# Paired weight chunks ordered by raw tile, and one reciprocal for two query blocks, in a hybrid convolution and attention layer

## The chip, the cores and the metric

The kernel runs on one core of a Trainium2 chip. A core has a matrix engine (TensorE, PE in the profile; its weight loads are shown apart as PEld), a vector engine (VectorE, DVE), a scalar engine (ScalarE, ACT), GpSimd (POOL), and SyncE (SP), which here only issues transfers (DMA). The metric is the time of one execution on the device in microseconds (us); lower is better.

## The reference

One layer over 512 latent tokens and 256 context tokens of width 1024, in float32. The input is normalised and modulated (h for the latent tokens, hc for the context), and one projection makes ten parts of width 1024:

```
parts = split(h @ w_in)            # b, c, x, z_a | q, k, v, z_b | g_a, g_b
y_a = (silu(z_a) * b * conv3(c * x)) @ w_out_conv
p   = softmax(concat([q.k_window * scale + bias, q.k_ctx * scale]))
y_b = (silu(z_b) * (p @ [v_window, v_ctx])) @ w_out_attn
y   = (sigmoid(g_a) * y_a + sigmoid(g_b) * y_b) @ w_o
out = x + gt * rmsnorm(y)
```

There are 16 heads of 64 channels. Each query sees a window of 8 x 16 grid positions and all context keys in one softmax.

## The kernel before

**Precision by splitting.** TensorE works on a rounded float type. Each operand is therefore split (`split`, line 64) into a high half, a cast on ScalarE (line 67), and the remainder, a subtraction on VectorE (line 68). A product is three matmuls: high by high, high by low, low by high.

**Weights.** A chunk of the input projection is 1024 x 256. It is loaded as two raw tiles of 512 KB (`Chunk`, line 84), the first with the rows 0 to 511, the second with the rows 512 to 1023. SP issues the two loads in this order (line 87). There are three buffers for raw tiles (`bufs=3`), so while one chunk has two of them, the next one can have only one of its tiles loaded; its other load waits until a buffer is free. The split halves go into tiles `w` (four buffers).

**Paired chunks.** Sixteen of the chunks are multiplied by a scheme with seven half-size products in place of eight. With b11 and b12 the left and right columns of the first raw tile, and b21 and b22 those of the second, it needs the splits of B11 = b11, B21 = b21, B22 = b22 and of four sums: T1 = b11 + b12, T2 = T1 + b22, T3 = b12 + b22, T4 = b21 + T2. The sums are made in place in the raw tiles: T1 and then T2 over b11, T4 over b21, T3 over b12. `first()` (line 96) does the four sums and splits B11, B21, T1 and T2. `second()` (line 110) splits T4, T3 and B22. T3 is the last that lies in the first raw tile; T4 and B22 lie in the second. `pair` (line 267) multiplies in the order B11, B21, T1, T2 (with A11, A12, X1, S2), then `chunk.more()` starts `first()` of the next paired chunk, and then T4, T3, B22 (with A22, S3, S4). Line 262 is every matmul of these products. Paired are the gate chunks zb 0 to 2, the convolution chunks cx and bz from 5 on, and all merge gates g but g2.

**Attention.** For each of 8 head pairs p, two heads h and four blocks b of 128 queries, `scores` (line 653) multiplies queries and keys (lines 664, 673), adds the bias and takes the extreme of the row (line 680, VectorE), then ScalarE takes the exponential with the sum of the row in z (line 686), VectorE the reciprocal of z (line 687), and ScalarE scales the block with it (line 688). Two blocks at a time, `turn2` (line 691) transposes them on TensorE (line 695) and splits them into TH and TL. `gather` (line 699) multiplies the four blocks of a head with the values (line 714).

**Order.** The loop at line 789 goes over the 64 blocks. In each step it takes some parts of the projections and gates of the plan (line 192) as filling for TensorE, then the scores two blocks ahead, and in every odd block the transposes of two. So the scores of a block stand in the program two steps ahead of its place, and the transposes of a pair stand behind its odd block. Outside the first stage (lines 405 to 514) the order on each engine is not written out by hand: it is planned when the program is built, from the order of the program and assumed durations of the instructions and transfers, and an engine then takes its queue in the planned order.

Of the kernel before, what the change touches and what calls it, by code (L numbers as in the profile page):

```python
# [9 lines left out]
F32 = mybir.dt.float32  # L10
F32R = mybir.dt.float32r
AF = mybir.ActivationFunctionType
# [3 lines left out]
P = 128  # L16
# [11 lines left out]
def layer(ctx: ExitStack, tc, xp, ctxt, ctxT, cc, wmod, small, wfirst, win, wout, wo, rel, tab, out):  # L28
    nc = tc.nc
# [34 lines left out]
    def split(H, L, src, scale=None):  # L64

        if scale is None:
            nc.scalar.copy(H, src)  # L67
            nc.vector.tensor_sub(L, src, H.bitcast(F32))  # L68
        else:
            nc.scalar.mul(H, src, scale)  # L70
            nc.vector.scalar_tensor_tensor(
                out=L, in0=src, scalar=scale, in1=H.bitcast(F32), op0=ALU.mult, op1=ALU.subtract
            )
# [4 lines left out]
    def wtile(shape):  # L78
        return wp.tile(shape, F32R, name="w", bufs=4)

    class Chunk:
# [14 lines left out]
        def first(self):  # L96
            (b11, b12), (b21, b22) = self.b = [(r[:, :, :P], r[:, :, P:]) for r in self.raws]
            t, sums = (wtile([P, 2, 2, 4, P]) for _ in range(2))
            for x, b in ((t[:, 0], b11), (t[:, 1], b21)):
                split(x[:, 0], x[:, 1], b)  # L100
            nc.vector.tensor_add(b11, b11, b12)
            split(sums[:, 0, 0], sums[:, 0, 1], b11)
            nc.vector.tensor_add(b11, b11, b22)
            split(sums[:, 1, 0], sums[:, 1, 1], b11)
            nc.vector.tensor_add(b21, b21, b11)
            nc.vector.tensor_add(b12, b12, b22)
            self.B = {"B11": t[:, 0], "B21": t[:, 1], "T1": sums[:, 0], "T2": sums[:, 1]}
            return self

        def second(self):  # L110
            t, last = (wtile([P, 2, 2, 4, P]) for _ in range(2))
            for n, x, b in (("T4", t[:, 0], self.b[1][0]), ("T3", t[:, 1], self.b[0][1]), ("B22", last[:, 0], self.b[1][1])):
                split(x[:, 0], x[:, 1], b)
                self.B[n] = x

# [151 lines left out]
    def pair(c1, c2):  # L267

        w = chunk().B
        a, b, e = (pj()[:, :256] for _ in range(3))  # L270
        first, second = slice(0, 256), slice(256, S)
        product(a, A11, w["B11"], True)
        nc.scalar.copy(c1[:, first], a)
        product(b, A12, w["B21"], True)
        product(e, blocks_h["X1"], w["T1"], True)
        nc.scalar.copy(c2[:, second], e)
        product(a, blocks_h["S2"], w["T2"], False)
        nc.scalar.copy(c2[:, first], a)
        nc.vector.tensor_add(c1[:, first], c1[:, first], b)  # L279
        chunk.more()  # L280
        yield
        product(b, A22, w["T4"], True)
        product(a, blocks_h["S3"], w["T3"], False)
        nc.scalar.copy(c1[:, second], a)
        product(e, blocks_h["S4"], w["B22"], False)
        for cols, x in ((second, c1[:, second]), (first, e)):
            nc.vector.scalar_tensor_tensor(
                out=c2[:, cols], in0=c2[:, cols], scalar=-1.0, in1=x, op0=ALU.mult, op1=ALU.subtract
            )
        nc.vector.tensor_add(c1[:, second], c1[:, second], b)  # L290
# [35 lines left out]
    with ExitStack() as p0:  # L326
# [44 lines left out]
        raws, first = {}, {}  # L371
# [33 lines left out]
        with tc.manual_schedule(engines={E.PE, E.DVE, E.Activation, E.SP}):  # L405
# [74 lines left out]
            for k in range(KT):  # L480
# [9 lines left out]
                m = st.tile([P, S], F32, name="m", bufs=2)  # L490
# [95 lines left out]
    aw = pa.enter_context(tc.tile_pool(name="aw", bufs=2, reuse_waits="tile"))  # L586
# [63 lines left out]

    def scores(p, h, b):
        qd, qe, ks = KQ[p]
        if b == 0:
            nc.sync.dma_start(bt[:, 2 * h:2 * h + 2], rel[p, h])
        s = psS()
        qs = slice(b * P, (b + 1) * P)
        if b < 3:

            t = ks[h][:, b * P:(b + 2) * P]
            kt = bass.AP(t.tensor, t.offset, [t.ap[0], [(4 - b) * P, 2], [1, 2 * P]])
            for n, lhs in enumerate((qd[h], qe[h])):
                nc.tensor.matmul(  # L664
                    s.rearrange("p (a c) -> p a c", a=2), lhsT=lhs[:, qs], rhs=kt, start=n == 0, stop=n == 1
                )
        else:
            kt = ks[h].rearrange("p (t c) -> p t c", c=P)
            s4 = s.rearrange("p (t c) -> p t c", c=P)
            n = 0  # L670
            for lhs in (qd[h], qe[h]):
                for o, i in ((slice(0, 2), slice(0, 4, 3)), (slice(2, 4), slice(4, 6))):
                    nc.tensor.matmul(
                        s4[:, o], lhsT=lhs[:, qs], rhs=kt[:, i], start=n == 0, stop=n == 3, skip_group_check=True
                    )
                    n += 1
        e = 2 * h + (b == 3)
        m = aw.tile([P, 1], F32, name="m", bufs=4)
        s3 = s.rearrange("p (a c) -> p a c", a=2)
        nc.vector.tensor_tensor_reduce(  # L680
            out=s3, in0=s3, in1=bt[:, e::4 - e][:, 0:2], scale=-1.0, scalar=3.0e38,
            op0=ALU.add, op1=ALU.min, accum_out=m,
        )
        pt = aw.tile([P, S], F32, name="pt", bufs=3)
        z = aw.tile([P, 1], F32, name="z", bufs=4)
        nc.scalar.activation(pt, s, AF.Exp, bias=m, scale=-1.0, accum_out=z)  # L686
        nc.vector.reciprocal(z, z)  # L687
        nc.scalar.mul(pt, pt, z)  # L688
        return pt

    def turn2(pts, b, TH, TL):
# [91 lines left out]
    pj.tags = (0, 1, 2)  # L783
    blocks = [(p, h, b) for p in range(NPAIR) for h in range(2) for b in range(4)]
    pts = {n: scores(*blocks[n]) for n in range(2)}
    T = None
    sums = block_sums()
    done = 0
    for i, (p, h, b) in enumerate(blocks):
        slot = i % 8  # L790
        if slot == 0:
            items = chain(*(g for g, _ in fill[p]))
            total, done = sum(n for _, n in fill[p]), 0
        if i in (4, 5, 6, 8, 9, 10, 12, 13):
            next(sums)
        upto = -(-total * (slot + 1) // 8)
        while done < upto:
            next(items)
            done += 1
        if T is not None and b == 0:  # L800
            gather(*T)
        if i + 2 < len(blocks):
            pts[i + 2] = scores(*blocks[i + 2])
        if b == 0:
            TH = aw.tile([P, 4, 4, P], F32R, name="TH", bufs=1)
            TL = aw.tile([P, 4, 4, P], F32R, name="TL", bufs=1)
            T = p, h, TH, TL

        if b % 2:
            turn2([pts.pop(i - 1), pts.pop(i)], b - 1, TH, TL)  # L810
# [41 lines left out]
    def quarter(name, pool, tags):  # L852
        return [pool.tile([P, 2, S], F32, name=f"{name}{q}", tag=t) for q, t in enumerate(tags)]
# [28 lines left out]
    for j in range(KT):  # L882
# [17 lines left out]
        if j == 4:  # L900
# [4 lines left out]
            for i in range(2):  # L905
                gb = cv.tile([P, S], F32, name="ta")
                ps = pj()
                for k in range(4):
                    n = 4 * i + k
# [3 lines left out]
        if j == 4:  # L913
            A11, S3 = operand("A11", hp, ("u2", "u3")), operand("S3", hp, ("a2", "a3"))
            for q in range(2):
                split(A11[q][:, 0], A11[q][:, 1], raws[q][:, :, h0])
                x = cv.tile([P, S], F32, name="tb").rearrange("p (k c) -> p k c", k=2)
# [3 lines left out]
            B22, B21, T2, T3 = (quarter(n, hp, (f"h{2 * i}", f"h{2 * i + 1}")) for i, n in enumerate(("B22", "B21", "T2", "T3")))  # L921
# [4 lines left out]
        if j == 6:  # L926
# [6 lines left out]
            T4 = B12  # L933
# [36 lines left out]
    def partial(t, n, first):  # L970
        d = sums[:, t, 3:4]
        if first:
            nc.vector.tensor_scalar(out=d, in0=sums[:, t, n:n + 1], scalar1=0.25 / D, scalar2=EPS, op0=ALU.mult, op1=ALU.add)
        else:
            nc.vector.scalar_tensor_tensor(out=d, in0=sums[:, t, n:n + 1], scalar=0.25 / D, in1=d, op0=ALU.mult, op1=ALU.add)
# [38 lines left out]
    t = [hp.tile([P, 2, S], F32R, name=f"wB22{i}", tag=f"h{2 + i}") for i in range(4)]  # L1014
# [119 lines left out]
```

## Time and profile before

| | us |
|---|---|
| median of 3 runs | 715.55 (715.27 to 716.63) |
| the profiled execution's own time | 715.21 |
| its span in the trace | 713.4 |
| TensorE busy in it | 699.3 |
| VectorE busy | 585.3 |
| ScalarE busy | 425.2 |
| GpSimd busy | 37.6 |

The span runs from the first instruction of the program to the end of the last; 1.8 us of the execution lie outside it. The granted clock of TensorE is 0.998 of the full one. The attention loop runs from about 137 to 512 us of the span, the merge gates from there to about 640 us, and the output product after that. An engine's idle time matters only where TensorE or the end waits for it. In the rows of the profile a line such as L106 is a line of the kernel before; where a helper makes all splits, its line (67 and 68) is told apart by the tiles, as `w<-raw` or `TL<-ps`.

### The profile page before, as it was taken

How to read it: one execution, taken by the hardware profiler on the slowest of the kernel's cores; microseconds unless marked ns; L12 is line 12 of the kernel's file. 1: busy time of each engine (PE TensorE's matmuls, PEld its weight loads, DVE VectorE, ACT ScalarE, POOL GpSimd, SP SyncE). 2: the span in 40 equal slices, each digit the busy share in tenths (PEclk: the TensorE clock that was granted, in tenths of full speed). 3: DMA queues.
4: the chain of work that ended last, by engine and by line, in shares of the span. 5: the costliest groups of instructions: out<-in, count | busy, mean ns of one | idle time of the engine just before them, and what ended most of it. 6: DMA issues, size and time to landing. Idle time of an engine off the chain costs nothing.

```text
span 713.4 us, 11043 instructions
## 1 busy us (share of the span) xinstructions
PE 699.3 (98%) x4052; PEld 614.0 (86%) x4052; DVE 585.3 (82%) x1139; ACT 425.2 (60%) x822; POOL 37.6 (5%) x78
## 2 busy tenths in 40 slices
PE   7999999999999999999999999999999999999996
PEld 4888888888888998898998999998888999988885
DVE  6999999985677897879888698999696675665996
ACT  6575643555476675675866657787673444342563
POOL 0000001120020200201102002000000000000000
PEclk9999999999999999999999999999999999999999
DMA  8996995454260452441563145212832333470013
GB/s 348 406 348 219 288 342 173 97 147 120 74 152 16 111 167 98 92 129 38 134 219 85 27 133 134 92 61 85 283 119 74 105 119 119 161 281 30 30 59 119
DMA packets 34905, 104.06 MB, mean 146 GB/s; under 512 B 4513, under 2 KB 4769, under 8 KB 34850
## 3 DMA queue, kind: packets, MB, share of 16 engines
q1 hardware_dynamic: 28946, 92.20, 37.9%
q0 software_dynamic: 5760, 11.01, 7.3%
q8 instruction: 32, 0.52, 0.3%
q14 instruction: 23, 0.19, 0.1%
q10 hardware_dynamic: 144, 0.13, 0.1%
HBM read 87.07 MB, written 5.24 MB: 129 GB/s over the span
## 4 chain that ended last, share of the span: by engine, by line
PE 89%; DVE 6%; DMA 3%; ACT 1%; issue 1%; DVEq 0%; SPq 0%; ACTq 0%
PE ps L262 17%; PE ps L143 13%; PE ps L144 13%; PE ps L145 13%; PE ps L156 6%; PE ps L941 5%; PE ps L714 4%; PE ps L695 3%; PE ps L161 3%; PE ps L664 2%; DMA raw<-in_win 2%; PE ps L169 2%; DVE w L68 2%; PE ps L397 2%; PE ps L401 2%; PE ps L398 2%
## 5 line engine op out<-in xcount | busy, mean ns | idle before, releaser
L67 ACT CAST w<-raw 128x512 fp32r<-128x512 f32 (+1 forms) x170 | 128.2, 767 | 89.7 <-PE ps L145 45.6
L68 DVE TENSOR_TENSOR w<-raw,w 128x512 fp32r<-128x512 f32 (+1 forms) x170 | 145.6, 866 | 39.5 <-ACT w L67 39.1
L143 PE MATMUL ps<-h,w 128*128 128x512 f32 x272 | 106.8, 392 | 0.0
L145 PE MATMUL ps<-h,w 128*128 128x512 f32 x272 | 106.2, 390 | 0.0
L144 PE MATMUL ps<-h,w 128*128 128x512 f32 x272 | 105.9, 390 | 0.0
L262 PE MATMUL ps<-S,w 128*128 128x256 f32 x768 | 97.4, 283 | 0.0
L262 PEld LDWEIGHTS ps<-S,w 128*128 128x128 f32 x768 | 94.5, 192 | 0.0
L262 PE MATMUL ps<-h,w 128*128 128x256 f32 x576 | 75.2, 284 | 0.2 <-DVE g L279 0.2
L262 PEld LDWEIGHTS ps<-h,w 128*128 128x128 f32 x576 | 71.9, 191 | 1.5 <-DVE g L279 0.5
L145 PEld LDWEIGHTS ps<-h,w 128*128 128x128 f32 x272 | 51.1, 188 | 10.8
L144 PEld LDWEIGHTS ps<-h,w 128*128 128x128 f32 x272 | 51.1, 188 | 10.4
L143 PEld LDWEIGHTS ps<-h,w 128*128 128x128 f32 x272 | 51.1, 188 | 10.3
L686 ACT ACTIVATE pt<-ps,m 128x512 f32<-128x512 f32 x64 | 44.1, 689 | 15.2 <-DVE m L680 14.1
L688 ACT ACTIVATE pt<-pt,z 128x512 f32<-128x512 f32 x64 | 45.8, 725 | 5.2 <-DVE z L687 5.0
L67 ACT CAST TH<-ps 128x512 fp32r<-128x512 f32 x64 | 35.5, 585 | 20.2 <-PE ps L695 20.0
L68 DVE TENSOR_TENSOR TL<-ps,TH 128x512 fp32r<-128x512 f32 x64 | 42.9, 679 | 3.1 <-ACT TH L67 2.9
L680 DVE CUSTOM_DVE_ANT_1 ps<-ps,bt 128x512 f32<-128x512 f32 x56 | 38.7, 694 | 4.1 <-PE ps L664 4.1
L695 PE MATMUL ps<-ident,pt 128*128 128x128 f32 x256 | 33.5, 273 | 0.8 <-DVE TL L68 0.8
L156 PE MATMUL ps<-w,h 128*128 128x512 f32 x128 | 32.5, 395 | 0.0
L695 PEld LDWEIGHTS ps<-ident,pt 128*128 128x128 f32 x256 | 29.2, 140 | 3.3 <-ACT pt L688 1.3
L714 PE MATMUL ps<-TL,V 128*128 128x256 f32 (+1 forms) x96 | 28.2, 323 | 2.4 <-DVE TL L68 2.4
L714 PE MATMUL ps<-TH,V 128*128 128x256 f32 (+1 forms) x96 | 28.5, 319 | 0.0
(247 smaller groups left out, 1337.6 us busy)
## 6 DMA issues: line engine op xcount, KB each, us to landing
raw<-in_win SPq DMA_DIRECT2D x74, 512.0 KB, 4.5
wm<-in_wmod SPq DMA_DIRECT2D x34, 512.0 KB, 6.4
raw<-in_wout SPq DMA_DIRECT2D x16, 512.0 KB, 3.6
bt<-in_rel SPq DMA_DIRECT2D x16, 256.0 KB, 3.4
B<-in_wo SPq DMA_DIRECT2D x8, 512.0 KB, 6.6
fraw<-in_wfirst SPq DMA_DIRECT2D x8, 384.0 KB, 7.9
qd<-qd POOLq DMA_DIRECT2D x24, 128.0 KB, 2.3
qe<-qe POOLq DMA_DIRECT2D x24, 128.0 KB, 3.4
```

Of the source, the lines that this page charges most:

```text
L67: nc.scalar.copy(H, src)
L68: nc.vector.tensor_sub(L, src, H.bitcast(F32))
L143: nc.tensor.matmul(ps, lhsT=H[k][:, cs], rhs=mH[k], start=k == 0, stop=False)
L144: nc.tensor.matmul(ps, lhsT=H[k][:, cs], rhs=mL[k], start=False, stop=False)
L145: nc.tensor.matmul(ps, lhsT=L[k][:, cs], rhs=mH[k], start=False, stop=k == KT - 1)
L156: nc.tensor.matmul(ps, lhsT=mH[k][:, ts], rhs=both[k].rearrange("p a c -> p (a c)"), start=k == 0, stop=False, skip_group_check=True,)
L262: nc.tensor.matmul(ps, lhsT=w[:, x, k], rhs=act[y][k], start=start and k + o == 0, stop=k == 3 and o == 2, skip_group_check=True,)
L680: nc.vector.tensor_tensor_reduce(out=s3, in0=s3, in1=bt[:, e::4 - e][:, 0:2], scale=-1.0, scalar=3.0e38, op0=ALU.add, op1=ALU.min, accum_o ...
L686: nc.scalar.activation(pt, s, AF.Exp, bias=m, scale=-1.0, accum_out=z)
L688: nc.scalar.mul(pt, pt, z)
L695: nc.tensor.transpose(tp[:, c], pt[:, c * P:(c + 1) * P], ident)
L714: nc.tensor.matmul(o3[:, dst], lhsT=V[p][:, kt, h], rhs=src(t), start=n == 0 and t is TH, stop=n == len(work) - 1 and t is TL,)
```

## The change

Three edits. In `first()` the work is ordered by raw tile: B11, the sum T1 and its split come first, then B21, the sum T2 and its split, and the sum for T3 comes ahead of that for T4. In `second()` T3 is split ahead of T4; the products that use them keep their order, T4 first. In `scores` the row sums of an even and the following odd block go into two columns of one tile z. One reciprocal after the odd block's exponential serves both, and then both blocks are scaled one after the other; the even block, which was scaled right after its own exponential, is now scaled there.

```diff
         def first(self):
             (b11, b12), (b21, b22) = self.b = [(r[:, :, :P], r[:, :, P:]) for r in self.raws]
             t, sums = (wtile([P, 2, 2, 4, P]) for _ in range(2))
-            for x, b in ((t[:, 0], b11), (t[:, 1], b21)):
-                split(x[:, 0], x[:, 1], b)
+            split(t[:, 0, 0], t[:, 0, 1], b11)
             nc.vector.tensor_add(b11, b11, b12)
             split(sums[:, 0, 0], sums[:, 0, 1], b11)
+            split(t[:, 1, 0], t[:, 1, 1], b21)
             nc.vector.tensor_add(b11, b11, b22)
             split(sums[:, 1, 0], sums[:, 1, 1], b11)
+            nc.vector.tensor_add(b12, b12, b22)
             nc.vector.tensor_add(b21, b21, b11)
-            nc.vector.tensor_add(b12, b12, b22)
...
         def second(self):
             t, last = (wtile([P, 2, 2, 4, P]) for _ in range(2))
-            for n, x, b in (("T4", t[:, 0], self.b[1][0]), ("T3", t[:, 1], self.b[0][1]), ("B22", last[:, 0], self.b[1][1])):
+            for n, x, b in (("T3", t[:, 0], self.b[0][1]), ("T4", t[:, 1], self.b[1][0]), ("B22", last[:, 0], self.b[1][1])):
                 split(x[:, 0], x[:, 1], b)
                 self.B[n] = x
...
         pt = aw.tile([P, S], F32, name="pt", bufs=3)
-        z = aw.tile([P, 1], F32, name="z", bufs=4)
-        nc.scalar.activation(pt, s, AF.Exp, bias=m, scale=-1.0, accum_out=z)
-        nc.vector.reciprocal(z, z)
-        nc.scalar.mul(pt, pt, z)
+        if b % 2 == 0:
+            z = aw.tile([P, 2], F32, name="z", bufs=4)
+            nc.scalar.activation(pt, s, AF.Exp, bias=m, scale=-1.0, accum_out=z[:, 0:1])
+            whole[:] = pt, z
+        else:
+            first, z = whole
+            nc.scalar.activation(pt, s, AF.Exp, bias=m, scale=-1.0, accum_out=z[:, 1:2])
+            nc.vector.reciprocal(z, z)
+            for i, x in enumerate((first, pt)):
+                nc.scalar.mul(x, x, z[:, i:i + 1])
         return pt
```

More of the change, by code (lines that the diff above doesn't have):

```diff
@@ L649, in keys_queries @@
         yield
+    whole = []
     def scores(p, h, b):
```

## The prediction

> **What bounds the kernel now.** I read the page first, for the share of each engine; then the busy time by stretches, for where TensorE (PE) is idle; then the waits; then the order of time around one idle place.
>
> ```profile
> span 713.4 us, 11043 instructions
> PE 699.3 (98%) x4052; PEld 614.0 (86%) x4052; DVE 585.3 (82%) x1139; ACT 425.2 (60%) x822; POOL 37.6 (5%) x78
> PE 89%; DVE 6%; DMA 3%; ACT 1%; issue 1%; DVEq 0%; SPq 0%; ACTq 0%
> ```
>
> TensorE is busy 699.3 of 713.4 us and is 89% of the chain that ended last. So at most 14.1 us could be won by any edit that leaves the matmuls alone, and only where TensorE stands still. The stretches (columns: stretch, its length, busy us of each engine with its count, granted clock, DMA share, GB/s) tell where that is:
>
> ```profile
> 242.00:258.00 16.00, 15.19 (x120) 14.44 (x119) 14.03 (x31) 13.20 (x29) 2.54 (x5) 1.00 0.58 139
> 340.00:356.00 16.00, 15.07 (x119) 14.34 (x119) 13.91 (x31) 13.08 (x30) 2.04 (x4) 1.00 0.53 125
> 436.00:453.00 17.00, 16.37 (x128) 15.54 (x127) 15.21 (x34) 14.28 (x30) 2.55 (x5) 1.00 0.55 138
> 480.00:510.00 30.00, 29.01 (x218) 27.19 (x217) 27.43 (x55) 23.87 (x46) 0.00 (x0) 1.00 0.39 134
> 510.00:640.00 130.00, 130.00 (x780) 116.43 (x779) 89.91 (x142) 62.74 (x103) 0.00 (x0) 1.00 0.44 152
> ```
>
> TensorE lacks 0.81, 0.93, 0.63 and 0.99 us in four stretches of the attention part, 3.36 us together, and nothing in the 130 us of merge gates, where five of the sixteen paired chunks are used. The clock is full, 1.00, in all of them. The waits name the cause (columns: total us, times, longest):
>
> ```profile
>   DVE raw L106: 6.8, 5
> PE ps L714 <- DVE TL L68: 2.4, 3, 0.9
> ```
>
> The first row stands under "who waited for it" of the raw tiles: the sum b12 + b22 (line 106) waited 6.8 us for loads of raw tiles, in five places. The second: TensorE's attention products (line 714) waited three times, 2.4 us, for TL. The first of the three places, in order of time (start, duration, instruction, in brackets its wait):
>
> ```profile
> 241.22 0.62 ACT L67 CAST w<-raw 128x512 fp32r<-128x512 f32 x1 [0.84 <-PE ps L174]
> 241.88 0.68 DVE L68 TENSOR_TENSOR w<-raw,w 128x512 fp32r<-128x512 f32 x1
> ...
> 243.14 1.14 ACT L67 CAST w<-raw 128x512 fp32r<-128x512 f32 x2
> ...
> 244.22 0.69 DVE L68 TENSOR_TENSOR w<-raw,w 128x512 fp32r<-128x512 f32 x1
> ...
> 244.93 1.31 SPq L87 DMA_DIRECT2D raw<-in_win  x2
> ...
> 246.87 0.69 DVE L101 TENSOR_TENSOR raw<-raw 128x512 f32<-128x512 f32 x1
> ...
> 248.96 1.68 PE L262 MATMUL ps<-h,w 128*128 128x256 f32 x12
> ...
> 249.39 0.69 DVE L106 TENSOR_TENSOR raw<-raw 128x512 f32<-128x512 f32 x1 [1.83 <-DMA raw<-in_win]
> ...
> 250.00 1.29 DVE L68 TENSOR_TENSOR w<-raw,w 128x512 fp32r<-128x512 f32 x2
> ...
> 251.21 0.68 DVE L103 TENSOR_TENSOR raw<-raw 128x512 f32<-128x512 f32 x1
> 251.81 0.69 DVE L680 CUSTOM_DVE_ANT_1 ps<-ps,bt 128x512 f32<-128x512 f32 x1
> ...
> 252.41 0.69 DVE L105 TENSOR_TENSOR raw<-raw 128x512 f32<-128x512 f32 x1
> ...
> 253.62 0.15 DVE L687 RECIPROCAL z<-z 128x1 f32<-128x1 f32 x1
> 253.69 1.27 DVE L68 TENSOR_TENSOR TL<-ps,TH 128x512 fp32r<-128x512 f32 x2
> ...
> 255.01 0.50 PE L714 MATMUL ps<-TL,V 128*128 128x512 f32 x1 [0.81 <-DVE TL L68]
> ```
>
> Here `second()` of the chunk zb 0 splits T4 (241.22 and 241.88), then T3 and B22 (casts at 243.14, T3's remainder at 244.22). T3 is the last reader of that chunk's first raw tile, so the tile is free at 244.91 and SP issues the next chunk's second raw tile into it at 244.93. The next chunk (cx 5) has its first raw tile already: its sum of line 101 runs at 246.87. Line 106 is next on VectorE (DVE), wants the second tile, and holds the engine for 1.83 us until 249.39. From there VectorE works without a break up to TL, which ends at 254.96, and TensorE stands for 0.81 us. The other places:
>
> ```profile
> 339.28 0.68 DVE L68 TENSOR_TENSOR w<-raw,w 128x512 fp32r<-128x512 f32 x1
> ...
> 342.33 1.31 SPq L87 DMA_DIRECT2D raw<-in_win  x2
> 346.90 0.69 DVE L106 TENSOR_TENSOR raw<-raw 128x512 f32<-128x512 f32 x1 [1.95 <-DMA raw<-in_win]
> ...
> 444.10 0.69 DVE L106 TENSOR_TENSOR raw<-raw 128x512 f32<-128x512 f32 x1 [1.66 <-DMA raw<-in_win]
> ...
> 484.12 1.88 DVE L68 TENSOR_TENSOR w<-raw,w 128x512 fp32r<-128x512 f32 x3
> 485.47 21.88 SPq L87 DMA_DIRECT2D raw<-in_win  x7
> 486.39 1.69 PE L262 MATMUL ps<-h,w 128*128 128x256 f32 x12 [0.23 <-DVE g L279]
> ...
> 489.69 0.69 DVE L106 TENSOR_TENSOR raw<-raw 128x512 f32<-128x512 f32 x1 [0.88 <-DMA raw<-in_win]
> ...
> 494.32 0.63 PE L695 MATMUL ps<-ident,pt 128*128 128x128 f32 x4 [0.76 <-DVE TL L68]
> ```
>
> **The change part by part.** *T3 before T4 in* `second()`. No instruction is added. T3 takes the places that T4 has, so the first raw tile is free when the split of 241.88 ends, at 242.56, and not at 244.91. This load is the next in SP's queue and goes 0.02 us after the tile is free (244.91, 244.93), so it starts about 2.35 us earlier. From 244.93 to the wait's end at 249.39 are 4.46 us; begun 2.35 us earlier it lands near 247.0. VectorE comes to it at 247.56 (246.87 plus 0.69), so the 1.83 us wait goes, with some 0.5 us to spare. TL then ends 1.83 us earlier, near 253.1, while TensorE would come to line 714 at 254.20 (255.01 less 0.81): the whole 0.81 us goes. The place near 347 has the same shape (split of T4 until 339.96, load at 342.33), and I take it for the one near 444 too; their waits of 1.95 and 1.66 us are also below 2.35 us, so 0.93 and 0.63 us go. At the fourth place T4, T3 and B22 follow one another (three in 1.88 us, 0.63 each), so the load starts only 0.6 us earlier; of VectorE's 0.88 us 0.28 stay, and of TensorE's 0.76 us I count 0.6 as won. Its other 0.23 us, behind line 279, stays.
>
> What T4 loses: its remainder now ends where T3's did, 244.91, and TensorE begins the product with it at 248.96: 4.0 us of cover. The least cover is at the fourth place, 485.4 against 486.39, 1.0 us. So it costs nothing; where the cover were gone a place would cost 0.6 to 2.35 us. The earlier load is passed by nothing else: SP held it at its head.
>
> *The order by raw tile in* `first()`. The same four sums and four splits (a cast on ScalarE (ACT) and a remainder on VectorE each). T1's split now stands ahead of B21's, and the sum of line 106 behind line 103. Where a wait for the second tile is left, T1's remainder (half of the 1.29 us at 250.00) can now run in it. That is worth nothing where the wait is gone, and at most the 0.28 us of the fourth place; I count 0. It could lose only where the second tile comes first, and SP issues them in order.
>
> *One reciprocal for two blocks.* 64 become 32.
>
> ```profile
> L687 DVE RECIPROCAL z<-z 128x1 f32<-128x1 f32 x64 | 9.8, 155 | 1.3 <-ACT pt L686 1.2
> L688 ACT ACTIVATE pt<-pt,z 128x512 f32<-128x512 f32 x64 | 45.8, 725 | 5.2 <-DVE z L687 5.0
> L695 PEld LDWEIGHTS ps<-ident,pt 128*128 128x128 f32 x256 | 29.2, 140 | 3.3 <-ACT pt L688 1.3
> ```
>
> The next VectorE instruction starts 0.07 us behind a reciprocal (253.62, 253.69), so VectorE gets back 32 x 0.07 = 2.2 us. ScalarE's 5.0 us of waiting for reciprocals should about halve. Both lie beside TensorE's work except in the four chains above, which are closed already: 0. The Trainium skill ("VectorE: DVE Perf Modes", § The DRAIN you can't avoid) says that the next operation cannot issue until the pipe is empty. By that a reciprocal would cost its whole 155 ns, 5.0 us over 32; the row shows 0.07 us, and the sum stays the same by either.
>
> The price: the even block's scaling (line 688) now waits for the odd block's exponential, sum and reciprocal, and the odd block's own scaling follows it, 0.72 us later than now. The transposes of both stand behind the odd block in any case, so only a pair whose transposes follow at once can lose. TensorE's weight loads waited 1.3 us in all for scaled blocks, in the whole run; the one place where it shows:
>
> ```profile
> 200.76 0.60 PE L695 MATMUL ps<-ident,pt 128*128 128x128 f32 x4
> 201.03 0.72 ACT L688 ACTIVATE pt<-pt,z 128x512 f32<-128x512 f32 x1
> 201.80 0.66 PE L695 MATMUL ps<-ident,pt 128*128 128x128 f32 x4
> ```
>
> The even block's four transposes start at 200.76, before the odd block is scaled; now they cannot before 201.75, and the second four not before 202.5. With the queue left as it is that is 1.0 us; other matmuls that are ready can fill it, and then it is 0. I take 0.2, nearer to the filled case, since TensorE has other work at hand in 98% of the span.
>
> **The sum**, on the profiled execution's 715.21 us: 0.81 + 0.93 + 0.63 + 0.60 = 2.97 won, 0.2 lost, 2.8 net: 712.4. The median of the runs is 715.55, 0.34 above; so I say **712.8**. Its own range: 711.4 (all 3.36 us, and a quarter of the 3.3 us for which weight loads of line 695 stood) to 714.2 (the fourth place stays and the whole 1.0 us is lost: 1.37 won).
>
> **The rivals.** *The wait moves along with its load (no measurable change).* The order of each queue is planned at build, from an assumed duration of the load. The plan put line 106 at 247.56, where its data were 1.83 us away, so it takes loads for shorter than they are. If it now moves readers of the second tile forward by the same 2.35 us, VectorE or ScalarE stands as long, only earlier, and TL ends where it does now. The same holds if the plan still casts T4 first. For it: such a misjudgement is in the trace five times. Against: line 106 cannot pass line 101, which ends at 247.56, after the new landing. Time: 715.5, 715.0 to 716.2.
>
> *Late scaling starves TensorE (slower).* If the plan leaves the transposes close behind the odd block, TensorE waits one scaling, 0.72 us, in a pair. Once in each of the eight head pairs, 5.8 us, less 2.97 won: 718.4. It decides from the sixth such pair on (6 x 0.72 = 4.32, less 2.97 is 1.35, about what can be told, below). For it: the pair at 200.76, and ScalarE has 13.20 busy of 16 us in the crowded stretch, where two scalings in a row push back what follows. Against: 1.3 us of such waits in 256 transposes. The Trainium skill ("Perfetto Trace Analysis", § Optimizing Scalar/DVE Operations) speaks for this rival: where these engines are not saturated but cause bubbles elsewhere, breaking instructions up may finish work sooner, and grouping helps a saturated engine. VectorE has 82% of the span, 88% in the first stretch; no run here shows yet which holds.
>
> *More than the four gaps.* The freed VectorE time also takes 1.3 of the 3.3 us of line 695's weight loads: 715.55 less 3.36 and 1.3, 710.9. Against: most of those waits are hidden, since the matmuls of that line stand in no row above but the fourth place's.
>
> **How the numbers follow.** Forecast 0.56; wait moves along 0.21; slower 0.15; more won 0.08. A measurement of this kernel can tell about 0.2%, 1.4 us, from no change. Faster (below 714.1): 0.56 and 0.08, less 0.02 for the top of the forecast's own range: 0.62. Slower (above 717.0): 0.15. Same: 0.23. The range 711.2 to 716.8 leaves out most of the slower case and part of the largest gain, some 0.2.
>
> **What would show it.** Right: in the four places the load of the second raw tile starts right behind the first of `second()`'s three remainders, the two sums with b22 have no wait on a raw tile (at most 0.3 us at the fourth place), and TensorE is busy over 15.9 us of 16 around each. Of the reciprocal: 32 of them, ScalarE's wait for them near 2.5 us, and weight loads of line 695 waiting for scaled blocks below 2 us. Wrong: waits on raw tiles that stay near 6.8 us (first rival), or line 695 waiting for line 688's successor by over 4 us (second). The prediction fails too if TensorE's queue comes out in another order with new gaps elsewhere between 137 and 510 us.

## The result, and the profile after

The changed kernel takes 710.92 us (median of 5 runs, 710.50 to 712.37) against 715.55 us before. The ratio is 0.9934, with a 95% interval from 0.9919 to 0.9948: 4.6 us faster. The forecast had 2.8 us (712.8), and 711.2 as the low end of its range; the measured time lies below it. The direction, the place and the main cause were right. The size was too small.

The page of the changed kernel, its profiled execution (710.50 us, span 708.3):

```profile
span 708.3 us, 11048 instructions
PE 697.6 (98%) x4052; PEld 613.9 (87%) x4052; DVE 582.6 (82%) x1107; ACT 421.4 (59%) x822; POOL 37.6 (5%) x78
PE 97%; DMA 1%; DVE 1%; SPq 0%; ACT 0%; issue 0%; DVEq 0%; ACTq 0%
```

TensorE (PE) is now 97% of the chain that ended last (89% before), and it executes the same 4052 matmuls. VectorE (DVE) has 32 instructions fewer. The four stretches in which TensorE stood before (columns as in the prediction):

```profile
242.00:258.00 16.00, 16.00 (x129) 15.61 (x128) 15.38 (x31) 13.37 (x29) 2.42 (x5) 1.00 0.56 159
340.00:356.00 16.00, 16.00 (x129) 15.61 (x128) 15.20 (x32) 12.82 (x27) 2.04 (x4) 1.00 0.48 137
436.00:453.00 17.00, 17.00 (x137) 16.61 (x137) 16.37 (x35) 13.91 (x32) 1.93 (x4) 1.00 0.45 133
480.00:510.00 30.00, 30.00 (x214) 27.95 (x213) 23.59 (x47) 21.35 (x41) 0.00 (x0) 1.00 0.57 179
```

TensorE has no gap left in any of them. The first place in order of time, in the changed kernel. The changed lines have moved: line 100 is the sum for T1, 103 that for T2, 105 the one for T3 (106 before), 106 the one for T4; 694 is the reciprocal, 722 the attention products:

```profile
241.49 0.69 DVE L68 TENSOR_TENSOR w<-raw,w 128x512 fp32r<-128x512 f32 x1
...
242.20 12.94 SPq L87 DMA_DIRECT2D raw<-in_win  x3
...
247.69 0.69 DVE L100 TENSOR_TENSOR raw<-raw 128x512 f32<-128x512 f32 x1
...
248.57 1.68 PE L262 MATMUL ps<-h,w 128*128 128x256 f32 x12
...
248.90 0.69 DVE L105 TENSOR_TENSOR raw<-raw 128x512 f32<-128x512 f32 x1
...
250.10 0.68 DVE L68 TENSOR_TENSOR TL<-ps,TH 128x512 fp32r<-128x512 f32 x1
250.70 0.68 DVE L103 TENSOR_TENSOR raw<-raw 128x512 f32<-128x512 f32 x1
251.30 0.16 DVE L694 RECIPROCAL z<-z 128x2 f32<-128x2 f32 x1
251.38 0.67 DVE L68 TENSOR_TENSOR TL<-ps,TH 128x512 fp32r<-128x512 f32 x1
...
253.20 0.40 PE L722 MATMUL ps<-TL,V 128*128 128x512 f32 x1
```

T3's remainder is the first of the three, at 241.49. The load of the next chunk's second raw tile goes at 242.20, when before it went at 244.93. The sum for T3 runs at 248.90 without a wait, and TL is done at 252.05, over 1 us ahead of the product that needs it. Before, TensorE waited for TL until 255.01.

How far ahead the changed kernel is, step by step, can be read where the first product (B11) of a paired chunk starts. The starts before, for the chunks that follow one another round the four places:

```profile
241.96 1.22 PE L262 MATMUL ps<-h,w 128*128 128x256 f32 x9
256.77 1.48 PE L262 MATMUL ps<-h,w 128*128 128x256 f32 x11
354.27 1.96 PE L262 MATMUL ps<-h,w 128*128 128x256 f32 x15
451.48 1.72 PE L262 MATMUL ps<-h,w 128*128 128x256 f32 x13
530.36 1.83 PE L262 MATMUL ps<-h,w 128*128 128x256 f32 x14
```

The same five in the changed kernel:

```profile
241.56 1.70 PE L262 MATMUL ps<-h,w 128*128 128x256 f32 x13
255.31 1.94 PE L262 MATMUL ps<-h,w 128*128 128x256 f32 x15
351.62 2.06 PE L262 MATMUL ps<-h,w 128*128 128x256 f32 x16
447.92 1.82 PE L262 MATMUL ps<-h,w 128*128 128x256 f32 x14
525.27 1.96 PE L262 MATMUL ps<-h,w 128*128 128x256 f32 x15
```

The lead is 0.40, 1.46, 2.65, 3.56 and 5.09 us. So the four places gave 1.06, 1.19, 0.91 and 1.53 us, 4.69 together; 0.40 came before them, and nothing after (the spans differ by 5.1). The prediction had 0.81, 0.93, 0.63 and 0.60. In a second traced execution of the changed kernel (`after_2`, 711.10 us) the same starts give 1.06, 1.20, 0.90 and 1.34, and nothing ahead of the first place (241.98 against 241.96). So the 0.40 differs from one execution to the next and is not put down to the change.

The times of the two traced executions differ by less than their spans, 715.21 to 710.50, 4.7 us. The changed kernel spends 2.2 us outside its span, against 1.8 before. In all ten of its executions it is 2.1 to 2.2 us, and at most 1.9 in those of every other version below. The runs do not show why.

### The profile page after: what moved, and what is told of

The parts are those of the page before. It is cut to its first block, busy times and chain, and to the rows that moved or that the text cites. A ratio compares the mean times of both kernels' runs of the same rounds, so it can differ in the third digit from the quotient of the medians.

```text
span 708.3 us, 11048 instructions
## 1 busy us (share of the span) xinstructions
PE 697.6 (98%) x4052; PEld 613.9 (87%) x4052; DVE 582.6 (82%) x1107; ACT 421.4 (59%) x822; POOL 37.6 (5%) x78
## 4 chain that ended last, share of the span: by engine, by line
PE 97%; DMA 1%; DVE 1%; SPq 0%; ACT 0%; issue 0%; DVEq 0%; ACTq 0%
PE ps L262 23%; PE ps L143 13%; PE ps L144 13%; PE ps L145 13%; PE ps L156 6%; PE ps L949 5%; PE ps L722 4%; PE ps L703 4%; PE ps L161 3%; PE ps L666 3%; PE ps L169 2%; PE ps L397 2%; PE ps L401 2%; PE ps L398 2%; DMA fraw<-in_wfirst 1%; PE ps L174 1%
## 5 line engine op out<-in xcount | busy, mean ns | idle before, releaser
L696 ACT ACTIVATE pt<-pt,z 128x512 f32<-128x512 f32 x64 | 42.9, 722 | 3.0 <-DVE z L694 3.0
L689 ACT ACTIVATE pt<-ps,m 128x512 f32<-128x512 f32 x32 | 22.0, 689 | 14.0 <-DVE m L682 13.5
```

Source lines behind the costliest of these rows:

```text
L696: nc.scalar.mul(x, x, z[:, i:i + 1])
```

## The experiments

Three explanations stood against one another. **L**, the prediction's: the second raw tile is loaded too late, and T3's earlier split takes that away. **O**: the order in `first()` takes the sums with b22 out of the way of TL. **Z**: the saved reciprocals give VectorE the time. The three edits were run alone and in pairs. Each ratio is against the kernel before, on the same chip:

| T3 split first | order in `first()` | one reciprocal for two | median us | ratio, 95% interval |
|---|---|---|---|---|
| yes | | | 710.47 | 0.9931 (0.9918 to 0.9945) |
| | yes | | 715.82 | 1.0004 (0.9995 to 1.0013) |
| | | yes | 712.59 | 0.9963 (0.9950 to 0.9975) |
| yes | yes | | 710.40 | 0.9931 (0.9918 to 0.9944) |
| yes | | yes | 711.76 | 0.9949 (0.9935 to 0.9963) |
| | yes | yes | 713.21 | 0.9971 (0.9960 to 0.9982) |
| yes | yes | yes (the change) | 710.92 | 0.9934 (0.9919 to 0.9948) |

**T3 first, alone.**

```diff
-            for n, x, b in (("T4", ...), ("T3", ...), ("B22", ...)):
+            for n, x, b in (("T3", ...), ("T4", ...), ("B22", ...)):
```

> Of the change only the order in second(): T3 split ahead of T4. Theory L (the late load of the second raw tile makes the gaps, and T3's earlier split takes it away): the load starts about 2.35 us earlier at three places and 0.6 us at the fourth, the waits of line 106 fall from 6.8 us to below 1, and most of the gain of 4.6 us is here: 711.9 to 712.9. Rival O (the order in first() does it, since it takes the sums with b22 out of the way of TL): 715.0 to 715.9 here. Rival Z (the freed reciprocals do it): 715.0 to 715.9 here.

It gave 5.1 us, the whole gain of the change and half a microsecond more. The load at the first place, and the sum for T3 (line 106), in this kernel:

```profile
242.64 11.89 SPq L87 DMA_DIRECT2D raw<-in_win  x3
...
248.15 0.68 DVE L106 TENSOR_TENSOR raw<-raw 128x512 f32<-128x512 f32 x1
```

The load goes 2.3 us earlier and the sum does not wait. The stretches of the four places have no idle TensorE left. L holds for where the gain is; its size was again expected too small. VectorE's queue came out in another order here too: one half of TL (250.70) runs ahead of the sum for T4 (251.30), where before both halves ran behind it (252.41, 253.69). No run moves the load alone, with a fourth raw buffer say, so the earlier load and the new order are shown together.

**The order in** `first()`**, alone.**

```diff
-            for x, b in ((t[:, 0], b11), (t[:, 1], b21)):
-                split(x[:, 0], x[:, 1], b)
+            split(t[:, 0, 0], t[:, 0, 1], b11)
             nc.vector.tensor_add(b11, b11, b12)
             split(sums[:, 0, 0], sums[:, 0, 1], b11)
+            split(t[:, 1, 0], t[:, 1, 1], b21)
...
+            nc.vector.tensor_add(b12, b12, b22)
             nc.vector.tensor_add(b21, b21, b11)
-            nc.vector.tensor_add(b12, b12, b22)
```

> Of the change only the order in first(): T1's split ahead of B21's, the sum for T3 behind T2's split and ahead of the sum for T4. Theory L: the load stays as late as before (some 4.4 us behind T3's split), so a wait of 1 to 2 us for the raw tile stays at each place, on ScalarE or on VectorE; 714.5 to 715.9. Rival O: 711.0 to 713.0, since TL no longer stands behind those sums. Rival Z: 715.0 to 715.9.

Nothing was gained. The sum for T3, now line 105 and behind T2's in the program, still comes next after T1's sum (246.86) on VectorE, and waits longer:

```profile
249.80 0.69 DVE L105 TENSOR_TENSOR raw<-raw 128x512 f32<-128x512 f32 x1 [2.24 <-DMA raw<-in_win]
```

So this edit is not what gives the gain. The place in the program did not change the place in the queue, so the run does not test what another place in the queue would be worth.

**One reciprocal for two blocks, alone** (the third part of the diff above).

> Of the change only the reciprocal of two blocks in one. Theory L: 715.0 to 716.6, the 2.2 us of VectorE lie beside TensorE's work, and at most 1.0 us is lost where transposes follow the odd block at once. Rival O: the same. Rival Z: below 714, since each reciprocal not waited for lets VectorE and ScalarE come earlier to TL and to the scaling.

It gave 3.0 us, which Z expected (below 714) and neither L nor O did. The load goes as late as before, and yet the sum for T3 does not wait. At the first place:

```profile
245.02 1.82 SPq L87 DMA_DIRECT2D raw<-in_win  x2
...
250.10 0.69 DVE L103 TENSOR_TENSOR raw<-raw 128x512 f32<-128x512 f32 x1
...
250.71 0.69 DVE L106 TENSOR_TENSOR raw<-raw 128x512 f32<-128x512 f32 x1
...
252.58 1.27 DVE L68 TENSOR_TENSOR TL<-ps,TH 128x512 fp32r<-128x512 f32 x2
DMA to landing us min/median/max: 3.8/3.8/3.8
```

The queues came out in another order. Line 106 stands behind T2's sum (line 103) and other work fills the time until the tile is there; TL ends at 253.85, before 254.96. The last row is the time from issue to landing of this one load, 3.8 us, against 4.4 before.

**T4, B22, T3: T3 last.**

```diff
-            for n, x, b in (("T4", ...), ("T3", ...), ("B22", ...)):
+            for n, x, b in (("T4", ...), ("B22", ...), ("T3", ...)):
```

> The kernel before, with second() in the order T4, B22, T3: the first raw tile becomes free a split later than before. Theory L: the load starts 0.93 us later at three places and 0.6 us at the fourth, the waits of line 106 grow by as much, and with them the gaps of TensorE: 3 x 0.93 + 0.6 = 3.4 us, 718.0 to 719.4. Rivals O and Z: no change, 715.0 to 715.9.

It came to 715.27 us, ratio 1.0000 (0.9991 to 1.0008): no change, against what L expected. The load at the first place goes when it went before, at 244.93:

```profile
244.88 1.31 SPq L87 DMA_DIRECT2D raw<-in_win  x2
```

The expectation had left out that T4 and B22 together free the chunk's *other* raw tile. If the load takes whichever of the two is free first, it goes after the second split in either order with T4 first, and only T3 first frees a tile after one split. The time of the load fits this, but the trace does not name the buffers, so it is argued. L's account of the load is not contradicted.

**Both orders, without the merged reciprocal.**

> Both orders, of first() and of second(), with a reciprocal for each block. T3 first alone gave 5.1 us, the order in first() alone nothing. Theory L (the load): nothing to add, 710.0 to 711.2. If the order in first() is a gain that the late load hid, below 709.8; if it costs (it puts the sum for T3 behind T2's split, so the raw tile waits longer in a crowded queue), above 711.5.

It is 710.40 us: the order in `first()` adds nothing to T3 first.

**T3 first with the merged reciprocal.**

> T3 first, and one reciprocal for two blocks, without the order in first(). Alone they gave 5.1 and 3.0 us. Theory L: both take away the same waits for the raw tile, so they do not add: 710.0 to 711.2. If the reciprocal had a gain of its own beside these waits, the two would add to some 707.5 to 708.5.

It is 711.76 us. The two gains of 5.1 and 3.0 us do not add, and the merged form is worse than T3 first alone. The traced execution took 713.38 us, the longest of the five. In its chain of waits two late raw tiles are back, in the fourth stretch:

```profile
480.94 5.03 DMA raw<-in_win
...
493.99 4.88 DMA raw<-in_win
```

The starts of the first product, read as above, show why the gains do not add. What each place gave, in us against the kernel before, in one traced execution of each:

| | first | second | third | fourth |
|---|---|---|---|---|
| T3 first alone | 1.09 | 1.21 | 0.92 | 1.39 |
| merged reciprocal alone | 1.01 | 0.68 | 0.83 | -0.21 |
| both | 1.07 | 1.19 | 0.90 | -0.87 |

The merged form alone closes most of the same three gaps, and a gap can be closed only once. At the fourth place it gains nothing alone, and in this longest execution of both it takes away there what T3 first gives; in the changed kernel, with the order in `first()` as well, it does not.

**The order in** `first()` **with the merged reciprocal.**

> The order in first() and one reciprocal for two blocks, with T4 split first. The load is as late as before. If the 3.0 us of the reciprocal come from the queue order on VectorE and ScalarE (the readers of the second tile come later, with other work in front of them), the order in first() leaves them: 712.0 to 713.5. If they come from VectorE's time, the same. Above 714.5 would say that the gain of the reciprocal alone hangs on one lucky order.

It is 713.21 us, 2.2 us below the kernel before: the merged form keeps most of its 3.0 us here. That fits either reading of where they come from, the order of the queues or VectorE's saved time.

**Where the merged form's 3.0 us come from.** Two kernels keep 64 reciprocals. In the first, both of a pair stand in the program behind the odd block's exponential, and both scalings behind them:

```diff
+            nc.scalar.activation(pt, s, AF.Exp, bias=m, scale=-1.0, accum_out=z[:, 1:2])
+            for i, x in enumerate((first, pt)):
+                nc.vector.reciprocal(z[:, i:i + 1], z[:, i:i + 1])
+            for i, x in enumerate((first, pt)):
+                nc.scalar.mul(x, x, z[:, i:i + 1])
```

> The kernel before with 64 reciprocals, but both of a pair taken after the odd block's exponential, and both scalings behind them: the delay of the merged form without its saving. If the gain of the merged form (3.0 us) comes from where the scalings stand in the queues, so that other work fills the wait for the raw tile: 712.0 to 713.2. If it comes from the 32 reciprocals saved: 715.0 to 716.5.

It came to 716.56 us, ratio 1.0014 (1.0003 to 1.0025), and the waits of line 106 are those of before:

```profile
DVE raw L106 <- DMA raw<-in_win: 6.7, 5, 2.2
```

This did not separate the two readings: the even block's reciprocal depends on nothing of the odd block, and at the first place the two scalings still stand apart in ScalarE's queue. In the second kernel the delay is forced, by two reciprocals of both columns, one for each scaling:

```diff
+            y = [aw.tile([P, 2], F32, name=f"y{i}", bufs=2) for i in range(2)]
+            for i in range(2):
+                nc.vector.reciprocal(y[i], z)
+            for i, x in enumerate((first, pt)):
+                nc.scalar.mul(x, x, y[i][:, i:i + 1])
```

> As with one reciprocal for two blocks, but two such reciprocals are taken, one for each scaling: both scalings still wait for the odd block's sum, and VectorE has its 64 reciprocals. If the 3.0 us of the merged form come from the forced delay of the scalings, which sets another order of the queues: 712.0 to 713.5. If they come from the 32 instructions saved: 715.0 to 716.5.

It is 714.57 us, ratio 0.9992 (0.9983 to 1.0001): a third of the gain by the medians, and the interval reaches from nothing to 1.2 us. The executions lie far apart, six of the twelve from 713.54 to 714.15 and the others up to 716.15; the traced one took 715.58. In it, at the first place, the queue has the better order, with line 106 behind line 103, but the load took 4.5 us and ScalarE and VectorE wait for it all the same:

```profile
249.70 0.62 ACT L67 CAST w<-raw 128x512 fp32r<-128x512 f32 x1 [0.73 <-DMA raw<-in_win]
...
250.36 0.69 DVE L68 TENSOR_TENSOR w<-raw,w 128x512 fp32r<-128x512 f32 x1 [0.60 <-ACT w L67]
...
251.57 0.68 DVE L106 TENSOR_TENSOR raw<-raw 128x512 f32<-128x512 f32 x1
DMA to landing us min/median/max: 4.5/4.5/4.5
```

So the new order does not hold the whole gain by itself. What else does, the 32 instructions saved or the quicker load of the merged kernel, stays open; no run separates them.

**Only the sum for T3 moved**, out of `first()` to its split in `second()`:

```diff
-            nc.vector.tensor_add(b12, b12, b22)
...
+                if n == "T3":
+                    nc.vector.tensor_add(b, b, self.b[1][1])
                 split(x[:, 0], x[:, 1], b)
```

> The kernel before, with only the sum for T3 moved: from first() to second(), right ahead of T3's split. The load of the second raw tile is no earlier than before (0.6 us later). If the gaps come from where this sum stands in VectorE's queue, in front of TL and of all that needs only the first tile, they shrink or go: 711.5 to 713.5. If the late load alone decides, since the next reader of the second tile (T2's sum) then waits in its place: 715.0 to 717.0.

It is 715.65 us, ratio 1.0001 (0.9992 to 1.0009). The sum (line 113 here) was planned into its old place, right behind T1's sum, and waits there:

```profile
249.87 0.69 DVE L113 TENSOR_TENSOR raw<-raw 128x512 f32<-128x512 f32 x1 [2.09 <-DMA raw<-in_win]
```

So it does not test what the place in the queue is worth; that stays untested.

**The change without the merged reciprocal, beside the change.**

> Both orders with a reciprocal for each block, again beside the changed kernel on one chip: 710.0 to 710.7. If the merged reciprocal costs something in the changed kernel, this one is 0.3 to 0.8 us faster than it; if it is free, within 0.2.

> The changed kernel, for comparison with the one without the merged reciprocal on the same chip: 710.5 to 711.2.

On one chip the version with both orders and 64 reciprocals took 710.44 us (710.38 to 710.62), the whole change 711.10 us (710.38 to 711.44). All ten executions of the first lie at or below 710.62, and eight of the ten of the second above it. The merged reciprocal costs 0.5 to 0.7 us in the changed kernel, and leaving it out (or taking T3 first alone) gives the fastest version that was run. It is also the steadier one. More than half of the cost, some 0.35 us, is the longer time outside the span; the spans themselves differ by 0.2 to 0.3 us (medians 708.6 and 708.7 against 708.8 and 709.0).

## Why the prediction was right or wrong

*T3 ahead of T4, the load and its wait: right.* The load started right behind the first of the three remainders, and the waits went at the first three places. One duration in it was off: the load was taken to need as long as before, some 4.4 us, and to land near 247.0. It needed 3.3 us (242.20 to 245.5) in the changed kernel. Little hung on that: after 4.4 us it would have landed at 246.6, still ahead of the sum for T3 at 248.90.

*The size of each gap: wrong, and the largest error at the first three places.* The sum took TensorE's idle time from the profile, 0.81, 0.93 and 0.63 us. The rows of TensorE at the first gap before, which show the starts:

```profile
253.58 0.40 PE L664 MATMUL ps<-ks,qd 128*128 128x512 f32 x1
253.82 0.39 PE L664 MATMUL ps<-ks,qe 128*128 128x512 f32 x1
...
255.36 0.40 PE L714 MATMUL ps<-TH,V 128*128 128x512 f32 x1
```

Back to back, these matmuls start 0.24 us apart but are shown as 0.39 to 0.40 us long, so each overlaps the next. Two starts, from 253.82 over 255.01 to 255.36, took 1.54 us where 0.47 would have done. The gap cost 1.07 us, not 0.81, and the measured gain there is 1.06. The same working from the starts gives 1.18 and 0.89 at the other two places, where 1.19 and 0.91 were gained. Together the three terms were 0.79 us too small. The page of the profile says the same: TensorE's busy time fell from 699.3 to 697.6 us with the same matmuls, so about 1.7 us that were shown as busy had been standing still. The 3.36 us of idle time, which the prediction took for the most that the four stretches could give, was no upper bound. The Trainium skill ("Perfetto Trace Analysis", § Identifying the Most-Contended Engine) says that the busy share of matmuls is not a good measure of how close a kernel is to its roofline, because they are pipelined; this trace agrees that the share misleads, by those 1.7 us, and the idle time beside it suffers from the same.

*The fourth place: wrong.* Of its 0.99 us idle 0.60 was counted; 1.53 us were gained (1.34 in the second execution). The sum let the load start 0.6 us earlier and left 0.28 us of VectorE's wait. TensorE's scores just ahead of this place, before:

```profile
484.19 0.40 PE L664 MATMUL ps<-ks,qd 128*128 128x512 f32 x1
```

The load, the same scores and the sum for T3 in the changed kernel:

```profile
480.15 15.06 SPq L87 DMA_DIRECT2D raw<-in_win  x5
480.61 0.40 PE L666 MATMUL ps<-ks,qd 128*128 128x512 f32 x1
...
484.02 0.69 DVE L105 TENSOR_TENSOR raw<-raw 128x512 f32<-128x512 f32 x1
```

TensorE is 3.58 us ahead here, and the load 5.32 us (485.47 before). So the load starts 1.74 us earlier than TensorE's lead alone would make it, not 0.6, and the sum does not wait. The rest beyond the 0.6 us comes from VectorE, which begins the three remainders at 479.40, not 484.12: 1.1 us more than TensorE's lead. That this is owed to the 1.66 us wait taken from VectorE at the third place is argued, not shown. The prediction kept the old queue, let a remaining wait reach TensorE, and took the 0.23 us behind line 279 for a different matter. Both gaps are gone in this kernel and with T3 first alone.

*The sum.* It had 2.97 us won and 0.2 lost. The spans differ by 5.1: 0.79 more at the first three places, 0.93 more at the fourth, the 0.40 ahead of them, and no loss of 0.2.

*T4's cover: right.* Its product begins at 248.57, when T4 is long split, and no gap appeared there.

*The order in* `first()`*: right*, worth nothing by itself or on top of T3 first. Beside both other edits the medians differ by 0.8 us in its favour (710.92 against 711.76), but the intervals of the two ratios overlap.

*The merged reciprocal: the price was right in its place and wrong in the whole.* ScalarE now scales the pair in one go, at the place that was named as the dangerous one:

```profile
200.45 1.30 PE L156 MATMUL ps<-w,h 128*128 128x512 f32 x5
200.71 1.33 ACT L696 ACTIVATE pt<-pt,z 128x512 f32<-128x512 f32 x2
...
201.59 1.17 PE L703 MATMUL ps<-ident,pt 128*128 128x128 f32 x8
  PEld ps L703: 0.2, 1
```

The transposes start 0.16 us behind the first scaling's end (201.43), with other matmuls in front of them. The last row, under "who waited for it" of the scalings, says that weight loads waited 0.2 us for them in the whole run (1.3 before). So the 0.2 us in the sum was not lost here. ScalarE's wait for the reciprocals fell from 5.0 to 3.0 us; the prediction had 2.5. A reciprocal of two columns holds VectorE for 0.08 us (251.30 to the next start at 251.38), about the 0.07 us that the prediction read. But the part was costed as if it left the queues alone. Alone it moves the kernel by 3.0 us, and beside the two orders by 0.5 to 0.7 us the other way; neither was in the sum. The rule of the Trainium skill weighed there ("Perfetto Trace Analysis", § Optimizing Scalar/DVE Operations: breaking up may help where these engines only cause bubbles) does not fit the first of these; the second has its sign, but lies for the most part outside the span, where the rule says nothing.

*The rivals.* The wait did not move along with its load: the sums for T3 waited 0.5 us for raw tiles in place of 6.8, once, in the chunk ahead of the fourth place:

```profile
467.92 0.69 DVE L105 TENSOR_TENSOR raw<-raw 128x512 f32<-128x512 f32 x1 [0.47 <-DMA raw<-in_win]
```

Yet its mechanism is real. Where the load stayed late and the scalings were left alone, the planner put the sum for T3 behind T1's sum again, wherever the program had it (line 105, line 113), and it waited 2.1 to 2.2 us. Late scaling did not starve TensorE. "More than the four gaps" had nearly the right time, 710.9, by luck: the starts of the products rule its reason out, since all but 0.4 us of the lead arose at the four places.

## What to carry to other kernels

Where raw buffers are scarce, split first what frees a buffer soonest: one swapped pair of operations, on engines that were not the bound, gave 5 us. Cost a gap of TensorE by the starts of its matmuls, not by the idle time shown, which was about a quarter too small here. An edit that leaves the work alone but adds a dependence sets the order of the queues anew; two such gains need not add, since both may close the same gap, so each part is worth a run alone before all are kept.

## What the runs showed of the hardware that was not expected

The same load of 512 KB took different times in kernels that do the same work. The row of the page for these loads, before (74 issues, KB each, median us to landing), and in the kernel with T3 first alone:

```profile
raw<-in_win SPq DMA_DIRECT2D x74, 512.0 KB, 4.5
```

```profile
raw<-in_win SPq DMA_DIRECT2D x74, 512.0 KB, 3.8
```

At the first place it took 4.4 us before, with a second load 1.0 us behind it, and 3.3 us in the changed kernel and with T3 first alone, with the next load 4.0 and 3.3 us behind. The distance to the next load does not settle it: at the second place of the changed kernel (338.50) it took 4.5 us though the next load came 4.0 us later, and at the first place it took 3.8 us with the merged reciprocal alone and 4.5 us with two merged reciprocals, with 1.5 us to the next load in both. What sets the time of such a load stays open here.
